# P in a PSUM bank of its own and filled one step ahead, and ScalarE copying all of the solved values, in the scan of an RWKV-7 encoder

## The chip, the cores and the metric

The kernel runs on one core of a Trainium2 chip. The metric is the device time in microseconds (us) of one execution; three runs of the kernel before gave 3077.28, 3080.88 and 3091.75, so the median is 3080.88 us. Lower is better.

The core has five engines that run side by side, each through its own list of instructions in a fixed order: TensorE (PE in the rows; PEld is its weight load), VectorE (DVE), ScalarE (ACT), GpSimd (POOL), and SyncE (SP), which issues the DMAs. TensorE writes its results into PSUM, which has eight banks of 128 partitions by 512 fp32 values.

## The reference

Two encoder layers over two requests, a prompt of 512 tokens and a sample of 256, model width 1024. Layer 0 mixes with a window attention and a short convolution, layer 1 with a bidirectional RWKV-7 time mixing; after each come a cross-attention to 256 memory tokens and a SwiGLU. Only the time mixing of layer 1 is touched. Its core is a recurrence with a 64 x 64 state for each of 16 heads and two directions:

```
def wkv7_scan(r, w, k, v, a, b, reverse):
    def step(state, inp):
        rt, wt, kt, vt, at, bt = inp
        sa = jnp.einsum('bhij,bhj->bhi', state, at)
        state = state * wt[:, :, None, :] + sa[..., None] * bt[:, :, None, :] + vt[..., None] * kt[:, :, None, :]
        return state, jnp.einsum('bhij,bhj->bhi', state, rt)
    ...
for d in range(2):
    ...
    outs.append(wkv7_scan(r, decay, k_d, v, -kk, kk * a, reverse=(d == 1)))
y = outs[0] + outs[1]
```

## The kernel before

The scan is done by chunks of 64 tokens. Inside a chunk the recurrence is a triangular system that is solved by products; from chunk to chunk a state S is handed on. The work of the time mixing is cut into 12 units (L1113): eight of the prompt, each two heads over 512 tokens, and four of the sample, each four heads over 256 tokens. A unit goes through four generators: `prep` (L1158) makes the decayed keys and values, `inverse` (L1260) and `merge` (L1329) make the masked products of keys G and the inverses X, `scan` (L1358) runs the recurrence, `tail` (L1474) normalizes. `weave` (L1514) interleaves the scan of unit u with the inverse of u+1, the tail of u-1 and the prep of u+2.

A unit's scan has eight steps (four groups i, two steps j). Both directions are worked at once. In step (i, j):

- P (128 x 128, in PSUM) is the share of the values, four matmuls of G with uv (L1424), plus the share of the state, two matmuls of AR with S0 (L1427). The four go first and the first two of them start the sum.
- ScalarE copies P into R (L1431). Two matmuls multiply R by the inverse X into U (L1433), the solved values.
- U goes back into uv in two halves: ScalarE copies partitions 0 to 63 (L1434), then VectorE partitions 64 to 127 (L1435).
- Four matmuls of BT with uv give Z (L1442), and VectorE adds Z to the decayed state and so makes the next state S1 (L1447; L1449 in a first step). GpSimd decays that for the step after (L1466).
- Matmuls of uv with G and of S0 with AR add to the output y (L1453, L1457).

P, U and Z are slices of one PSUM tile C (L1419). All these matmuls are recorded in the helper `mm` (L1389), which is the line that rows give. The next step's P therefore starts only when C is free, and that is when VectorE has read Z.

PSUM is full: two banks for the matrix products that fill (pool `fmm`, L1585), two for the pool pg (its tiles g0 and g1), and one each for pc (C), pe, py and pp (L1586). In `inverse`, a group's eight matmuls of keys go alternately to g0 and g1 (L1273), and VectorE multiplies each bank by a mask into G (L1276). Two products of the inverse and two of the merge use g1 and g0 in turn.

What keeps TensorE busy beside the chain of a step is a generator `fill` (L1532): dense matrix products of layer 0's feed-forward and of the time mixing's own projections (L342 to L344), poured in by `pour` (L1373) three times in a step, at a rate that the table FILL (L31) sets for each unit. The order of each engine's list is not written out: a scheduler takes instructions when its own model says that their inputs are there, and `urgent` (L1382) gives those of the chain the highest priority. A change of a few lines so gives a new order for the whole stretch.

Of the kernel before, what the change touches and what calls it, by code (L numbers as in the profile page):

```python
# [9 lines left out]
F32 = mybir.dt.float32  # L10
# [29 lines left out]
class Net:  # L40
# [1067 lines left out]
    def mixer1_scan(self, L, Ld, rkv, zs, bvs, fill):  # L1108

        nc, a, ph = self.nc, self.a, self.ph  # L1110
# [8 lines left out]
        NG = 4  # L1119
# [140 lines left out]
        def inverse(u, o):  # L1260
# [4 lines left out]
            st = steps[units[u][0]]  # L1265
            for i in range(NG):
                gt = ph.tile([128, 2, 2, 2, 128], F32, name="G", bufs=7)
                ps = [self.pg.tile([128, 2, 2, 128], F32, name=f"g{h}") for h in range(2)]
                for j in range(2):
                    for d in range(2):  # L1270
                        c = st[2 * i + j][d]
                        for h in range(2):
                            nc.tensor.matmul(ps[h][:, j, d, :], lhsT=flat(BK[d][lohi[h], c]), rhs=flat(AR[d][lohi[h], c]),  # L1273
                                             start=True, stop=True)
                for h in range(2):
                    nc.vector.tensor_mul(gt[:, :, h], ps[h], self.tri.unsqueeze(1).to_broadcast([128, 2, 2, 128]))  # L1276
                o["G"].append(gt)
                for q in range(4):
                    d, f = q // 2, (q % 2) * 32
                    qs = slice(32 * q, 32 * q + 32)  # L1280
                    nc.scalar.copy(XL[qs, 4 * i:4 * i + 4, :].rearrange("p (s h) i -> p s h i", h=2),
                                   gt[qs, :, :, d, 64 * d + f:64 * d + f + 32])
                yield
# [11 lines left out]
            for k in range(14, 0, -1):  # L1295
                n = 15 - k
# [6 lines left out]
            for a in range(2):  # L1303
# [7 lines left out]
            o["Y"] = Y  # L1311
            four = lambda v: ((slice(32 * q, 32 * q + 32), G[v // 4][32 * q:32 * q + 32, v // 2 % 2, v % 2, q // 2, 32 * q:32 * q + 32],
                               (32 * q, 32 * q)) for q in range(4))
            ps = self.pg.tile([128, 16, 32], F32, name="g1")
            for v in range(16):
                for qs, g, at in four(v):
                    nc.tensor.matmul(ps[qs, v, :], lhsT=g, rhs=X1[qs, v, :], start=True, stop=True, tile_position=at)
            nc.scalar.copy(Y, ps)
            yield
            ps = self.pg.tile([128, 16, 32], F32, name="g0")  # L1320
            for v in range(16):
                for qs, g, at in four(v):
                    nc.tensor.matmul(ps[qs, v, :], lhsT=Y[qs, v, :], rhs=XL[qs, v, :], start=True, stop=True, tile_position=at)
# [5 lines left out]
        def merge(u, o):  # L1329

            X1, G, Y = o["X1"], o["G"], o["Y"]
            X = o["X"]
            for q in (1, 3, 0, 2):
                qs = slice(32 * q, 32 * q + 32)
                nc.scalar.copy(X[qs, :, qs], XL[qs])
            yield
            yield
            ps = self.pg.tile([128, 16, 32], F32, name="g1")
            for v in range(16):
                i, j, h = v // 4, v // 2 % 2, v % 2  # L1340
                for d in range(2):
                    nc.tensor.matmul(ps[quart(d, 1), v, :], lhsT=G[i][quart(d, 0), j, h, d, quart(d, 1)],
                                     rhs=X1[quart(d, 0), v, :], start=True, stop=True,
                                     tile_position=(64 * d, 64 * d + 32))
            for d in range(2):
                nc.scalar.copy(Y[quart(d, 1)], ps[quart(d, 1)])
            yield
            ps = self.pg.tile([128, 16, 32], F32, name="g0")
            for v in range(16):
                for d in range(2):  # L1350
                    nc.tensor.matmul(ps[quart(d, 0), v, :], lhsT=Y[quart(d, 1), v, :],
                                     rhs=X[quart(d, 1), v, quart(d, 1)], start=True, stop=True,
                                     tile_position=(64 * d + 32, 64 * d))
            for d in range(2):
                nc.scalar.copy(X[quart(d, 0), :, quart(d, 1)], ps[quart(d, 0)])
            yield

        def scan(u, o):  # L1358
# [51 lines left out]
            fresh = [True, True]  # L1410
            nxt = ahead(0)
            yield
            for i in range(NG):
                uv, bt = nxt
                for j in range(2):
                    s0, s1, ch, before, after = st[2 * i + j]
                    cd = (s0, s1)
                    S0 = state.get(ch)
                    C = self.pc.tile([128, 384], F32, name="C")  # L1419
                    P, U, Z = C[:, 0:128], C[:, 128:256], C[:, 256:384].rearrange("p (d v) -> p d v", d=2)  # L1420
                    with urgent():
                        for h in range(2):
                            for d in range(2):
                                mm(P[lohi[d], lohi[h]], G[i][:, j, h, d, lohi[d]], uv[:, j, d, lohi[h]], h == 0)  # L1424
                        if before:
                            for d in range(2):
                                mm(P[lohi[d]], AR[d][:, cd[d], d, :], S0[:, d, :])  # L1427
                    pour()
                    with urgent():
                        R = ph.tile([128, 128], F32, name="R", bufs=1)  # L1430
                        nc.scalar.copy(R, P)  # L1431
                        for h in range(2):
                            mm(U[:, lohi[h]], X[:, 4 * i + 2 * j + h, :], R[:, lohi[h]])  # L1433
                        nc.scalar.copy(uv[lohi[0], j, 0, :], U[lohi[0]])  # L1434
                        nc.vector.tensor_copy(uv[lohi[1], j, 1, :], U[lohi[1]])  # L1435
                    pour()
                    yield
                    with urgent():
# [110 lines left out]
    def mixer1(self, l=1):  # L1549
        tc, nc = self.tc, self.nc  # L1550
        with tc.tile_pool(name="spill", bufs=1, space=bass.MemoryType.DRAM) as dram:
# [23 lines left out]
            with tc.tile_pool(name="lora", bufs=1, side="right") as lora, \  # L1575
# [4 lines left out]
                with tc.tile_pool(name="tail", bufs=1, side="right", reuse_waits="tile") as self.tl, self.phase(), ExitStack() as c:  # L1580
# [2 lines left out]
                    L[1].update(Ld[1])  # L1583
                    pool = lambda name, bufs: c.enter_context(tc.tile_pool(name=name, bufs=bufs, space=PSUM, reuse_waits="tile"))
                    f.pmm = f.psm = pool("fmm", 2)  # L1585
                    for n in ("pg", "pc", "pe", "py", "pp"):  # L1586
                        setattr(self, n, pool(n, 1))
                    y = self.mixer1_scan(L, Ld, rkv, zs, bvs, self.fill(l, f, xsave, rkv, L, zs))

# [158 lines left out]
```

## Time and profile before

| what | value |
|---|---|
| median of three runs | 3080.88 us |
| the profiled execution | 3081.32 us, its span 3079.5 us |
| mean granted TensorE clock | 0.967 of full speed |
| TensorE busy (matmul) | 2920.3 us, 95% of the span |
| VectorE busy | 1731.7 us, 56% |
| ScalarE busy | 1303.3 us, 42% |
| GpSimd busy | 679.5 us, 22% |

The page has TensorE busy nearly everywhere, so the few places where it is idle, and what ended each idle time, tell more than the shares. A busy TensorE is not one at its peak: matmuls overlap and their ends are modelled, and at a granted clock of 0.5 the same work takes longer. The steps of the scan stand between 1370 and 2275 us: the last value copies start at 2272 us.

### The profile page before, as it was taken

The numbers are of one execution on the slowest core, as the hardware profiler recorded it, in microseconds if no ns is written. First come the engines' busy times: TensorE is split into PE (matmuls) and PEld (weight loads), VectorE is DVE, ScalarE is ACT, GpSimd is POOL, SyncE is SP. The second block draws the span as 40 slices with busy tenths as digits, with TensorE's granted clock in tenths as the row PEclk, the third lists the DMA queues.
The fourth block names the chain that finished last, engine by engine and source line by source line (L and its number), as shares of the span: only waits on it lengthen the run. The fifth ranks groups of instructions, "written<-read, shape, count | busy, mean of one in ns | idle before, by whom it ended". The sixth has DMA issues, their size and how long they took to land. (4 is left out here: it accounts for less than half of the span.)

```text
span 3079.5 us, 56085 instructions
## 1 busy us (share of the span) xinstructions
PE 2920.3 (95%) x22616; PEld 2494.0 (81%) x22616; DVE 1731.7 (56%) x3074; ACT 1303.3 (42%) x2588; POOL 679.5 (22%) x672
## 2 busy tenths in 40 slices
PE   7999999999999989889989999999989999999997
PEld 6888888888888878778877877777778888888886
DVE  8888647464354586455566556555436464334244
ACT  3333435242232376455555666556445332122122
POOL 3123004010000110232356334445345010000001
PEclk9999999999999999989886998999999999999999
DMA  4234332111365767754433654222352211212121
GB/s 126 57 84 134 111 126 84 62 56 55 108 203 186 225 194 245 234 175 145 139 107 93 188 172 119 78 78 87 115 185 71 66 42 63 75 55 69 55 69 55
DMA packets 367843, 353.45 MB, mean 115 GB/s; under 512 B 43616, under 2 KB 296672, under 8 KB 367584
## 3 DMA queue, kind: packets, MB, share of 16 engines
q1 hardware_dynamic: 367584, 349.88, 36.7%
q8 instruction: 177, 2.90, 0.4%
q14 instruction: 82, 0.67, 0.1%
HBM read 272.21 MB, written 72.88 MB: 112 GB/s over the span
## 5 line engine op out<-in xcount | busy, mean ns | idle before, releaser
L342 PE MATMUL mm<-xs,whi 128*128 128x512 f32 x2128 | 748.4, 354 | 13.2 <-ACT whi L271 11.1
L343 PE MATMUL mm<-xs,whi 128*128 128x512 f32 x2128 | 752.5, 354 | 2.8 <-DVE xs L230 2.3
L344 PE MATMUL mm<-xs,wlo 128*128 128x512 f32 x2128 | 747.5, 352 | 4.2 <-DVE wlo L272 4.1
L271 ACT CAST whi<-wraw 128x512 fp32r<-128x512 f32 (+1 forms) x492 | 301.9, 616 | 841.5 <-PE mm L343 789.0
L272 DVE TENSOR_TENSOR wlo<-wraw,whi 128x512 fp32r<-128x512 f32 (+1 forms) x492 | 365.6, 745 | 393.0 <-ACT whi L271 373.6
L342 PEld LDWEIGHTS mm<-xs,whi 128*128 128x128 f32 x2128 | 403.6, 190 | 71.0 <-ACT whi L271 11.5
L344 PEld LDWEIGHTS mm<-xs,wlo 128*128 128x128 f32 x2128 | 402.1, 189 | 61.6 <-DVE wlo L272 5.7
L343 PEld LDWEIGHTS mm<-xs,whi 128*128 128x128 f32 x2128 | 403.7, 190 | 57.3 <-DVE xs L230 3.2
L194 POOL TENSOR_TENSOR acc<-acc,sq 128x768 f32<-128x768 f32 (+2 forms) x72 | 114.6, 1592 | 1264.0 <-issue 896.0
L343 PE MATMUL mm<-fb,thi 128*128 128x256 f32 (+1 forms) x720 | 234.3, 326 | 1.2 <-issue 1.0
L342 PE MATMUL mm<-hid,whi 128*128 128x512 f32 (+1 forms) x528 | 186.1, 355 | 2.3 <-ACT hid L226 2.3
L343 PE MATMUL mm<-hid,whi 128*128 128x512 f32 (+1 forms) x528 | 187.6, 356 | 0.0
L344 PE MATMUL mm<-hid,wlo 128*128 128x512 f32 (+1 forms) x528 | 186.2, 354 | 0.0
L303 ACT CAST thi<-traw 128x512 fp32r<-128x512 f32 (+1 forms) x202 | 122.8, 610 | 128.2 <-PE mm L343 51.8
L342 PE MATMUL mm<-fb,thi 128*128 128x256 f32 x528 | 166.0, 315 | 10.1 <-ACT thi L303 9.3
L344 PE MATMUL mm<-fb,tlo 128*128 128x256 f32 x528 | 159.7, 304 | 10.5 <-DMA tlo<-low 8.0
L343 PEld LDWEIGHTS mm<-fb,thi 128*128 128x128 f32 x720 | 144.8, 201 | 5.7 <-DVE fb L227 0.5
L342 PE MATMUL mm<-fa,thi 128*128 128x512 f32 (+1 forms) x304 | 125.4, 414 | 3.6 <-ACT fa L226 1.2
L342 PEld LDWEIGHTS mm<-fb,thi 128*128 128x128 f32 x528 | 107.4, 204 | 18.2 <-ACT thi L303 12.5
L344 PEld LDWEIGHTS mm<-fb,tlo 128*128 128x128 f32 x528 | 107.0, 203 | 18.0 <-DMA tlo<-low 10.5
L344 PE MATMUL mm<-fa,tlo 128*128 128x512 f32 (+1 forms) x304 | 111.7, 368 | 2.6 <-DMA tlo<-low 2.6
L342 PEld LDWEIGHTS mm<-hid,whi 128*128 128x128 f32 x528 | 99.5, 189 | 17.7 <-ACT hid L226 2.7
(386 smaller groups left out, 5830.1 us busy)
## 6 DMA issues: line engine op xcount, KB each, us to landing
wraw<-in_ffn_wgu_dram SPq DMA_DIRECT2D x44, 1024.0 KB, 5.2
tlo<-low SPq DMA_DIRECT2D x128, 256.0 KB, 3.6
low<-wlo SPq DMA_DIRECT2D x120, 256.0 KB, 3.0
wraw<-in_ffn_wdown_dram SPq DMA_DIRECT2D x23, 1024.0 KB, 5.2
traw<-in_ffn_wgu_dram SPq DMA_DIRECT2D x56, 256.0 KB, 4.0
wraw<-in_ab_w_in_dram SPq DMA_DIRECT2D x24, 512.0 KB, 3.9
wraw<-in_ca_wkv_dram SPq DMA_DIRECT2D x8, 1024.0 KB, 5.5
kvd<-kv SPq DMA_DIRECT2D x32, 256.0 KB, 2.0
```

The source lines that it names most:

```text
L194: nc.gpsimd.tensor_add(acc, acc, sq)
L271: nc.scalar.copy(hi[:, :, :m], raw[:, k0:k1, j:j + m])
L272: nc.vector.tensor_sub(lo[:, :, :m], raw[:, k0:k1, j:j + m], hi[:, :, :m].bitcast(F32))
L303: nc.scalar.copy(hi[:, :n], raw[:, :n])
L342: nc.tensor.matmul(ps[:, s0:s1], lhsT=wh, rhs=xh[:, s0:s1], start=start and k == 0, stop=False)
L343: nc.tensor.matmul(ps[:, s0:s1], lhsT=wh, rhs=xl[:, s0:s1], start=False, stop=False)
L344: nc.tensor.matmul(ps[:, s0:s1], lhsT=wl, rhs=xh[:, s0:s1], start=False, stop=stop and k == n - 1)
```

## The change

P leaves the tile C and gets a pool pP with one bank. The four matmuls of the values' share are put into a function `part0` and are issued one step ahead, behind the two matmuls that make U, so that at the turn of a step only the two matmuls of the state's share are left. The bank comes from pool pg, which now has one tile name, g: a group's eight matmuls of keys go in two lots of four, each followed by its masking multiply, and all products of the inverse and the merge share that bank. Both halves of U are copied by ScalarE. In the code after, `mm` is L1388, `part0` L1412 to L1418, and the copies are L1435 (R), L1438 and L1439 (uv).

```
@@ inverse
             for i in range(NG):
                 gt = ph.tile([128, 2, 2, 2, 128], F32, name="G", bufs=7)
-                ps = [self.pg.tile([128, 2, 2, 128], F32, name=f"g{h}") for h in range(2)]
-                for j in range(2):
-                    for d in range(2):
-                        c = st[2 * i + j][d]
-                        for h in range(2):
-                            nc.tensor.matmul(ps[h][:, j, d, :], lhsT=flat(BK[d][lohi[h], c]), rhs=flat(AR[d][lohi[h], c]),
+                for h in range(2):
+                    ps = self.pg.tile([128, 2, 2, 128], F32, name="g")
+                    for j in range(2):
+                        for d in range(2):
+                            c = st[2 * i + j][d]
+                            nc.tensor.matmul(ps[:, j, d, :], lhsT=flat(BK[d][lohi[h], c]), rhs=flat(AR[d][lohi[h], c]),
                                              start=True, stop=True)
-                for h in range(2):
-                    nc.vector.tensor_mul(gt[:, :, h], ps[h], self.tri.unsqueeze(1).to_broadcast([128, 2, 2, 128]))
+                    nc.vector.tensor_mul(gt[:, :, h], ps, self.tri.unsqueeze(1).to_broadcast([128, 2, 2, 128]))
@@ inverse and merge, in four places (g1 or g0 before)
-            ps = self.pg.tile([128, 16, 32], F32, name="g1")
+            ps = self.pg.tile([128, 16, 32], F32, name="g")
@@ scan
             nxt = ahead(0)
             yield
+            def part0(i, j, uv):
+
+                P = self.pP.tile([128, 128], F32, name="P")
+                for h in range(2):
+                    for d in range(2):
+                        mm(P[lohi[d], lohi[h]], G[i][:, j, h, d, lohi[d]], uv[:, j, d, lohi[h]], h == 0)
+                return P
+            P = part0(0, 0, nxt[0])
             for i in range(NG):
...
-                    C = self.pc.tile([128, 384], F32, name="C")
-                    P, U, Z = C[:, 0:128], C[:, 128:256], C[:, 256:384].rearrange("p (d v) -> p d v", d=2)
+                    C = self.pc.tile([128, 256], F32, name="C")
+                    U, Z = C[:, 0:128], C[:, 128:256].rearrange("p (d v) -> p d v", d=2)
                     with urgent():
-                        for h in range(2):
-                            for d in range(2):
-                                mm(P[lohi[d], lohi[h]], G[i][:, j, h, d, lohi[d]], uv[:, j, d, lohi[h]], h == 0)
                         if before:
                             for d in range(2):
                                 mm(P[lohi[d]], AR[d][:, cd[d], d, :], S0[:, d, :])
...
                         for h in range(2):
-                            mm(U[:, lohi[h]], X[:, 4 * i + 2 * j + h, :], R[:, lohi[h]])
+                            mm(U[:, lohi[h]], X[:, 4 * i + 2 * j + h, :], R[:, lohi[h]], h == 0)
                         nc.scalar.copy(uv[lohi[0], j, 0, :], U[lohi[0]])
-                        nc.vector.tensor_copy(uv[lohi[1], j, 1, :], U[lohi[1]])
+                        nc.scalar.copy(uv[lohi[1], j, 1, :], U[lohi[1]])
+                        if j == 0:
+                            P = part0(i, 1, uv)
+                        elif i + 1 < NG:
+                            P = part0(i + 1, 0, nxt[0])
@@ mixer1
-                    for n in ("pg", "pc", "pe", "py", "pp"):
+                    for n in ("pg", "pP", "pc", "pe", "py", "pp"):
                         setattr(self, n, pool(n, 1))
```

The built lists show where the change puts these instructions. First TensorE in the scan of a prompt unit, before, at the turn of a step (C is the step's tile, uv its values, S the state, ar the decayed keys; mm, fa and thi are fill):

```order
L343 MATMUL mm_15593<-fa_11438,thi_15582 128x256
L344 MATMUL mm_15593<-fa_11438,tlo_15583 128x256
L1389 MATMUL C_15632<-uv_15451,G_14134 64x64 x4
L1389 MATMUL C_15632<-S1_11408,ar0_13201 64x128
L1389 MATMUL C_15632<-S1_11408,ar1_13696 64x128
L342 MATMUL mm_15639<-fa_11437,thi_15596 128x256
```

The same step of the same unit after, where its U is made (C from R and the inverse Xinv) and the step after next to it (P_15683):

```order
L1404 MATMUL e_15810<-ident_149,bk1_13709 128x128
L1388 MATMUL C_15660<-R_15677,Xinv0_11405 128x64 x2
L1388 MATMUL P_15683<-uv_15478,G_14151 64x64 x4
L342 MATMUL mm_15688<-fa_11440,thi_15666 128x256
L343 MATMUL mm_15688<-fa_11440,thi_15666 128x256
L344 MATMUL mm_15688<-fa_11440,tlo_15667 128x256
```

The four matmuls of the values' share stood between the state and the state's share; now the next step's four stand right behind U. Next VectorE before, in front of the copy of that same step's values (xr, lt2 and lane belong to the inverse of the next unit, fa and fb to the fill, kka and bk to the prep):

```order
L448 TENSOR_TENSOR fa_11443<-fa_11443,mm_15659 128x256
L1304 TENSOR_SCALAR lane_15359<-xr_15361,lanes_11363 128x16x16 x2
L448 TENSOR_TENSOR fa_11444<-fa_11444,mm_15673 128x256
L1234 SCALAR_TENSOR_TENSOR kka_16008<-th_15972,kk_15100 128x512
L1305 STREAM_TRANSPOSE XL0_11404<-lane_15359 128x16x2x16
L227 TENSOR_TENSOR fb_15904<-fa_11443,fb_15904 128x256
L300 TENSOR_TENSOR traw_15935<-traw_15935,gmu_11342 128x512
L1235 SCALAR_TENSOR_TENSOR bk1_15968<-kka_16008,cu_15630 128x8x64
L1435 COPY uv_15451<-C_15632 64x128
```

And ScalarE after, around the two copies of the same values:

```order
L226 CAST fb_15923<-fa_11445 128x256
L1405 COPY BT_15809<-e_15810 128x512
L226 CAST fb_15929<-fa_11446 128x256
L1438 COPY uv_15478<-C_15660 64x128
L1439 COPY uv_15478<-C_15660 64x128
L191 ACTIVATE sq_15926<-fa_11445 128x256
```

The second half of the values has left VectorE's queue and stands directly behind the first half on ScalarE. Last TensorE after, where two lots of matmuls of keys (g_16568 and g_16662) follow each other in the one bank of pool pg, with little between them:

```order
L1273 MATMUL g_16568<-ar1_15999,bk1_15998 128x128
L1388 MATMUL y_16421<-G_15090,uv_16422 64x64 x2
L1388 MATMUL C_16700<-uv_16422,BT_16428 64x64 x4
L1388 MATMUL y_16421<-G_15090,uv_16422 64x64 x2
L1388 MATMUL y_16421<-ar0_14292,S0_11410 128x64
L1388 MATMUL y_16421<-ar1_14817,S0_11410 128x64
L1273 MATMUL g_16662<-ar0_15390,bk0_15389 128x128
```

The same place before has the two lots in different banks:

```order
L1273 MATMUL g1_16530<-ar0_15364,bk0_15363 128x128
L1273 MATMUL g1_16530<-ar1_15969,bk1_15968 128x128
L1273 MATMUL g1_16530<-ar0_15364,bk0_15363 128x128
L1273 MATMUL g1_16530<-ar1_15969,bk1_15968 128x128
L1273 MATMUL g0_16629<-ar0_15364,bk0_15363 128x128
```

Before, a lot in g1 is followed by one in g0; now each lot needs the bank that the masking multiply of the lot ahead has to leave first.

## Rows read from the trace of the kernel before

**Rows 1.** busy us (count) by engine, two stretches; then clock, DMA share, GB/s

```profile
1370.00:2275.00 905.00, 842.69 (x10711) 696.36 (x10708) 504.92 (x1110) 515.21 (x1216) 371.26 (x423) 0.92 0.39 116
2275.00:3079.00 804.00, 775.95 (x4506) 679.84 (x4504) 371.06 (x502) 226.86 (x386) 96.91 (x72) 0.98 0.23 73
```

**Rows 2.** TensorE's waits, 1370 to 2275 us: total us, times, longest

```profile
PE C L1389 <- DVE uv L1435: 24.8, 21, 5.6
PE C L1389 <- DVE S L1447: 11.0, 10, 2.3
PE y L1389 <- ACT uv L1434: 4.2, 8, 0.8
...
PE C L1389 <- ACT Xinv L1355: 2.9, 1, 2.9
...
PE C L1389 <- ACT R L1431: 2.0, 4, 1.0
```

**Rows 3.** VectorE in a late step: start us, us, operation

```profile
1578.95 1.74 DVE L300 TENSOR_TENSOR traw<-traw,gmu 128x512 f32<-128x512 f32 x1
1580.62 1.21 DVE L1235 SCALAR_TENSOR_TENSOR bk<-kka,cu 128x512 f32<-128x512 f32 x1
1581.86 0.29 DVE L1435 COPY uv<-C 64x128 f32<-64x128 f32 x1
```

**Rows 4.** ScalarE in the same stretch

```profile
1576.00 0.25 ACT L1434 COPY uv<-C 64x128 f32<-64x128 f32 x1
```

**Rows 5.** TensorE in the same stretch, with the idle time before and its releaser

```profile
1576.30 0.34 PE L1389 MATMUL y<-G,uv 128*64 128x64 f32 x4 [0.83 <-ACT uv L1434]
1582.21 0.38 PE L1389 MATMUL C<-uv,BT 128*64 128x64 f32 x2 [5.58 <-DVE uv L1435]
```

**Rows 6.** all engines, another step, in order of time

```profile
1845.34 0.72 ACT L1252 ACTIVATE kh<-th,par 128x512 fp32r<-128x512 f32 x1 [2.17 <-POOL th L1249]
1845.96 0.24 ACT L1434 COPY uv<-C 64x128 f32<-64x128 f32 x1
...
1846.88 0.29 DVE L1435 COPY uv<-C 64x128 f32<-64x128 f32 x1
...
1847.23 0.59 PE L1389 MATMUL C<-uv,BT 128*64 128x64 f32 x6 [2.93 <-DVE uv L1435]
```

**Rows 7.** groups, 1370 to 2275 us: count | busy, mean ns | idle, releasers

```profile
L1273 PEld LDWEIGHTS g<-ar,bk 64*128 64x128 f32 x704 | 85.2, 212 | 18.3 <-issue 10.2 <-DVE G L1276 0.9 <-DVE w2l L1192 0.7
...
L1276 DVE TENSOR_TENSOR G<-g,tri 128x512 f32<-128x512 f32 x88 | 58.8, 688 | 56.1 <-PE g L1273 52.7 <-PE y L1389 2.7
...
L1447 DVE TENSOR_TENSOR S<-C,Sd 64x128 f32<-64x128 f32 x128 | 36.8, 288 | 33.4 <-PE C L1389 30.7
...
L1435 DVE COPY uv<-C 64x128 f32<-64x128 f32 x96 | 28.3, 295 | 86.6 <-ACT uv L1434 84.5
...
L1431 ACT COPY R<-C 128x128 f32<-128x128 f32 x95 | 24.8, 261 | 68.6 <-PE C L1389 68.0
...
L1434 ACT COPY uv<-C 64x128 f32<-64x128 f32 x96 | 24.5, 255 | 42.5 <-PE C L1389 42.3
```

**Rows 8.** TensorE at the turn of a step, in order of time

```profile
1504.32 0.45 PE L1389 MATMUL C<-uv,G 128*64 128x64 f32 x8 [1.35 <-DVE S L1447]
1504.57 0.42 PE L1389 MATMUL C<-S,ar 128*64 128x128 f32 x4
```

**Rows 9.** TensorE's fill matmuls behind the wait that ended at 1582 us

```profile
1584.29 0.41 PE L343 MATMUL mm<-fa,thi 128*128 128x256 f32 x1
1584.50 0.41 PE L344 MATMUL mm<-fa,tlo 128*128 128x256 f32 x1
```

**Rows 10.** TensorE's fill matmuls later

```profile
1602.01 0.28 PE L343 MATMUL mm<-fb,thi 128*128 128x256 f32 x1
1602.13 0.28 PE L344 MATMUL mm<-fb,tlo 128*128 128x256 f32 x1
```

**Rows 11.** the engines around that wait, columns as in Rows 1

```profile
1580.00:1604.00 24.00, 19.04 (x378) 16.47 (x380) 13.88 (x25) 9.13 (x20) 10.50 (x16) 0.70 0.25 68
```

More of the change, by code (lines that the diff above doesn't have):

```diff
@@ L1319, in inverse @@
             yield
-            ps = self.pg.tile([128, 16, 32], F32, name="g0")
+            ps = self.pg.tile([128, 16, 32], F32, name="g")
             for v in range(16):
@@ L1337, in merge @@
             yield
-            ps = self.pg.tile([128, 16, 32], F32, name="g1")
+            ps = self.pg.tile([128, 16, 32], F32, name="g")
             for v in range(16):
@@ L1347, in merge @@
             yield
-            ps = self.pg.tile([128, 16, 32], F32, name="g0")
+            ps = self.pg.tile([128, 16, 32], F32, name="g")
             for v in range(16):
```

## The prediction

> **What bounds the kernel now.** I read the busy time by stretches first. In the 905 us that hold the steps of the scan, TensorE is busy 842.7 us, so it is idle for 62.3; VectorE and ScalarE are busy 505 and 515 us, a little over half [rows 1]. TensorE is the engine that sets the end, and the list of its work is nearly the same after the change. What an edit in the scan can give directly is therefore some part of those 62 us, or a better granted clock: the mean there is 0.92, against 0.98 in the 804 us behind it [rows 1].
>
> Then I read who ended TensorE's idle time. The largest entry by far is VectorE's copy of the second half of the solved values: 21 waits, 24.8 us, the longest 5.6. Next come VectorE's state addition with 11.0 us in 10 waits, and ScalarE's copies with 4.2 (values), 2.9 (inverse) and 2.0 (R) [rows 2].
>
> Then the timeline of the longest wait, to see why the copy is late. ScalarE's half starts at 1576.00 and takes 0.25 us [rows 4]; VectorE's half starts only at 1581.86 [rows 3], and TensorE, which had run out of work at 1576.63, goes on at 1582.21 [rows 5]. VectorE was not waiting: other work stood in front of the copy, the last two pieces with 1.74 and 1.21 us [rows 3]. So the copy is not slow (295 ns on average [rows 7]); its queue is long. In another step ScalarE's half is itself late, behind a 0.72 us activation, and VectorE's copy adds less than a microsecond to a wait of 2.93 [rows 6].
>
> **The change part by part.** Times are against the profiled execution, 3081.32 us (span 3079.5), which is 0.44 above the median of the runs.
>
> *The second half of the values goes to ScalarE.* 96 copies of 295 ns leave VectorE, 28.3 us in all, and 96 of some 255 ns come to ScalarE, where they stand directly behind the first half in the built order; 96 x 0.255 is 24.5 us [rows 7]. In the longest wait the second half would then end at 1576.00 + 0.25 + 0.26 = 1576.51 in place of 1582.15, before TensorE needs it, and all 5.58 us go [rows 3 to 5]. In the other step it would end at 1846.46 in place of 1847.17: 0.7 of 2.93 us go and 2.2 stay [rows 6]. Done so for the 21 waits, 16.9 us go. Bounds: nothing, and all 24.8. I take -17.
>
> *What that does to the other users of the two engines.* ScalarE gets 5% more work in this stretch, and TensorE's waits on it are 4.2 + 2.9 + 2.0 = 9.1 us [rows 2]. If they grow in proportion that is half a microsecond; if each of the 96 copies delayed something that TensorE waits for at once, it is 24.5. I take +2, near the low end, because ScalarE is busy 515 of 905 us. VectorE loses 5.6% of its work; its state additions, 11.0 us of waits, gain between 0 and 11, and I take -1.
>
> *The values' share of P moves one step ahead.* Its matmuls took 0.25 us between the wait for the state and the first matmul of the state's share [rows 8]. The work stays on TensorE and so costs the same where TensorE is not idle. Where it waits, at the state (10 times), at the values (what is left of 21) or at R (4 times), 0.25 us of work now stands ahead of the wait, or is off the chain behind it. That is worth at most 35 x 0.25, about 8.8 us, and nothing where another wait comes next. I take -2. The state's share no longer needs the bank that VectorE reads Z from, but that read is the addition which makes the state, so no wait is added or taken there. The next P needs the bank that R was copied from, and U, which stands in front of it, has waited for R already: no new wait.
>
> *One bank for the products of keys.* There are two lots of four matmuls to each group, 96 lots in all, and each has to wait until the mask multiply of the lot ahead has left the bank. That multiply takes 0.69 us [rows 7]; with the hand-over I count 0.73. Before, a wait for it cost TensorE's weight loads 0.9 us in the whole stretch [rows 7], since eight matmuls could go before a bank came round. In the built order there are mostly a dozen or more other matmuls between two lots, some microseconds of work; in eleven places at most seven rows of the list, as in those shown with the change. Bounds: 0, and 96 x 0.73 = 70 us if every turn lay open. I take +1, since the scheduler has put work between and the nearest row, 0.9, is a wait for the same multiply. The inverse's and the merge's products already need the copy of the product ahead as their input, so one bank costs them nothing.
>
> *The clock.* Behind the 5.58 us wait, fill matmuls of 256 columns start 0.21 us apart [rows 9], where later they start 0.12 apart [rows 10]: TensorE ran at 1.2 GHz for about 16 us and then again at 2.4. The 24 us around it have a mean granted clock of 0.70 and 19.0 us of busy TensorE [rows 11]. With that wait gone I expect the drop to go as well, which is worth some half of 16 us; the other waits are shorter and I put no more on them. Other drops in this stretch come without such a wait and will fall anew in another order. A mean of 0.92 over 905 us is 145 us at the lower level [rows 1]; half of that lost again or won is 36 us either way. I take -6.
>
> Sum: -17 + 2 - 1 - 2 + 1 - 6 = -23 us, and 3081.3 - 23 = 3058.
>
> **Rivals.** *The wait moves to ScalarE (no change).* For it: ScalarE's queue makes the first half late too [rows 6], its waits for U's matmuls and its own busy time are as large as VectorE's, and a new order brings waits of its own; 24.8 us spread over 21 steps can come back as many small ones. Against it: VectorE's delays in the long wait come from instructions of over a microsecond [rows 3], and the two copies on ScalarE follow each other. If three quarters of the 23 us come back, the time is 3075.
>
> *The single bank of keys sets the pace (slower).* Its place is TensorE's list in the inverse, its price 0.73 us a turn when VectorE is free, and VectorE is busy 505 of 905 us [rows 1], so a multiply may start late. If two thirds of the 96 turns lay open, that is +47, and with the -23 of the rest the time is 3105. It decides from about a third open (23 us). Against it stand the matmuls that the order puts between the lots and the 0.9 us of now [rows 7]. Beside this: the Trainium skill, in PSUM — Partial Sum Buffer, Summary: rules for kernel authors, says to give matmuls a different bank from the one that is being read; by that rule alone the change takes away in the inverse what it gives to P. TensorE: Matmul & The Clock Gate, A second HAM failure mode: psum-queue depth-cycling, tells of a kernel in which cycling through banks left small idle times between groups of matmuls and the clock fell again and again. By that, the open turns would cost clock as well; the drop in the rows above followed one long wait, so the trace before neither bears it out nor excludes it.
>
> *The clock gains more.* If the stretch got 0.96 where it has 0.92, 36 us would go in place of the 6 that I count: 3058 - 30 = 3028. For it: long waits and a drop stand together in the trace [rows 5, 9]. Against it: only one wait is that long.
>
> *The change doesn't do what it says* is excluded by the order: the four matmuls stand behind U, and the copies stand together.
>
> **How the numbers follow.** A measurement of this kernel can tell about 0.5% (15 us) from no change. Chances: the forecast 0.50 (3043 to 3070, centre 3058), the wait that moves 0.29 (3068 to 3090), the bank 0.11, the clock 0.10. Faster by over 0.5% means below 3065.5: nearly all of the clock's 0.10 and 0.43 of the forecast, 0.53. Slower by over 0.5% means above 3096.3: 0.10 of the bank's and 0.01 of the rest, 0.11. Within 0.5%: 0.36. For 8 in 10 the range has to take in most of the forecast and of the moved wait and the nearer half of the clock: 3030 to 3090.
>
> **What would show it.** In the profile after, the entry of TensorE's waits for the second copy of the values (now on ScalarE) should be at most 8 us in the stretch of the steps, and the idle total below 45. Waits of the keys' matmuls or their weight loads on the mask multiply should stay under 3 us; 20 or more would be the bank. The state addition's waits should stay near 10. TensorE's busy time should fall only where the granted clock rises; the mean clock of the stretch should be 0.92 or more. I am wrong if ScalarE's copies become the largest wait with 15 us or more, or if the clock falls below 0.90 and eats what the waits gave.

## The result, and the profile after

The change made the kernel slightly slower. Its median is 3106.39 us over 19 runs (3087.38 to 3113.12), that of before 3084.36 over 19 runs on the same chip; the ratio is 1.0071 with a 95% interval of [1.0055, 1.0088]. The forecast was 3058 and faster; the time lies above its range too. A second set of runs of the unchanged kernel gave 1.0079 [1.0056, 1.0103].

The profiled execution took 3087.38 us (span 3085.6), the fastest of the 19, so its trace shows only 6 of the 22 us that the medians are apart. The same stretch of steps as in [rows 1], same columns:

```profile
1370.00:2275.00 905.00, 856.14 (x10666) 708.55 (x10662) 488.17 (x1011) 542.90 (x1299) 363.32 (x419) 0.92 0.39 115
2280.00:3085.00 805.00, 776.53 (x4512) 680.92 (x4510) 368.40 (x502) 228.35 (x388) 96.38 (x72) 0.98 0.23 73
```

TensorE's idle time fell from 62.3 to 48.9 us, but its busy time rose from 842.7 to 856.1 at the same clock of 0.92, and the stretch is longer in spite of that. The waits of TensorE after, 1370 to 2280 us (total us, times, longest), against [rows 2]:

```profile
PE P L1388 <- DVE S L1455: 10.7, 11, 2.4
PE g L1316 <- DVE X L1306: 7.0, 4, 2.3
PE mm L342 <- ACT fa L226: 3.3, 2, 2.1
PE C L1388 <- ACT Xinv L1354: 3.2, 3, 2.6
...
PE y L1388 <- ACT uv L1438: 2.8, 6, 0.9
...
PE C L1388 <- ACT R L1435: 2.5, 5, 0.8
PE g L1273 <- DVE G L1275: 1.5, 2, 1.1
```

The 24.8 us for the second copy are gone: its line, now L1439, ends no wait. The state addition stands where it was, and the mask multiply, which now has to free the only bank of keys, costs 1.5 us. New is the wait for X, which VectorE makes for the inverse; with the copy alone and two banks it is 5.8 us (e1_act_copy below), so it is not the single bank's. The idle total stays above the 45 us that the forecast named as a sign. So the waits did for the most part what was forecast, and the time did not. The busy time says where to look: groups of TensorE over the whole execution (count | busy us, mean ns | idle, releasers), first before, then after.

```profile
L1273 PE MATMUL g<-ar,bk 64*128 64x128 f32 x768 | 113.4, 319 | 0.0
L1389 PE MATMUL C<-R,Xinv 128*128 128x64 f32 x384 | 59.7, 280 | 5.0 <-ACT Xinv L1355 2.9 <-ACT R L1431 2.0
L1389 PE MATMUL C<-uv,G 128*64 128x64 f32 x768 | 45.9, 242 | 13.8 <-DVE S L1447 11.0 <-DVE uv L1435 1.8
```

```profile
L1273 PE MATMUL g<-ar,bk 64*128 64x128 f32 x768 | 123.3, 303 | 2.0 <-DVE G L1275 1.5 <-ACT Xinv L1354 0.3
L1388 PE MATMUL C<-R,Xinv 128*128 128x64 f32 x384 | 61.3, 285 | 5.7 <-ACT Xinv L1354 3.2 <-ACT R L1435 2.5
L1388 PE MATMUL P<-uv,G 128*64 128x64 f32 x768 | 47.3, 242 | 0.4 <-ACT R L1435 0.4
```

A row counts two passes of the array for each of these fp32 matmuls, so the 384 matmuls of keys stand as x768. The keys' matmuls (g) are as many as before and each is no longer, yet together they keep TensorE 10 us longer. Busy time counts neighbours that lie over each other once, so a part of the same work no longer does. I also added up, from 1240 us to the last copy of y, the time from each matmul's start to the next one's, less idle time, and gave it to the first of the two, at whatever clock was granted there. By that TensorE's work is 948.4 us before and 969.5 after: keys 106.1 to 116.1, U 44.8 to 54.1, the values' share 29.3 to 39.3, 29 us in all, of which other groups give back 8. I call such sums work below; these three terms were to be explained.

**Keys.** The two row halves of a keys' tile (h = 0 uses rows 0 to 63 of the array, h = 1 rows 64 to 127) went to two banks before. A lot of eight passes in one half, after, and the instruction behind it (start us, us):

```profile
1385.51 1.16 PE L1273 MATMUL g<-ar,bk 64*128 64x128 f32 x8
1386.60 0.50 PE L1142 MATMUL e<-la,w2h 128*128 128x512 f32 x1
```

Sixteen passes, before, where the list mixes the two halves in places:

```profile
1388.06 1.98 PE L1273 MATMUL g<-ar,bk 64*128 64x128 f32 x16
1389.96 0.39 PE L342 MATMUL mm<-fa,thi 128*128 128x256 f32 x1
```

Eight passes of one half take 1.09 us to the next start, 0.136 each; sixteen mixed ones took 1.90, less than twice 1.09. In the trace before, 127 of the 662 times that a pass of keys follows another of keys, it starts within 80 ns of it, on average by 8: two halves run at the same time. After there is not one in 663.

**U and the share.** The values' share behind U, after:

```profile
1490.86 0.55 PE L1388 MATMUL C<-R,Xinv 128*128 128x64 f32 x4
1491.34 0.45 PE L1388 MATMUL P<-uv,G 128*64 128x64 f32 x8
1491.72 0.39 PE L342 MATMUL mm<-fa,thi 128*128 128x256 f32 x1
```

U before, followed by fill:

```profile
1490.24 0.55 PE L1389 MATMUL C<-R,Xinv 128*128 128x64 f32 x4
1490.61 0.36 PE L342 MATMUL mm<-fb,thi 128*128 128x256 f32 x1
```

U to the next start is 0.37 us before and 0.48 after; the share is 0.25 before, with the state's share behind it [rows 8], and 0.38 after. Together 0.62 became 0.86. The third column names the part of the array that a matmul uses: U and the fill use 128*128, the share 128*64. Before, the share's neighbour behind it used 128*64 too; after, it stands between two 128*128, and each change of that form costs time. The whole stretch agrees: at the full clock a pass of U takes 107 ns on average to the next start when a 128*128 comes next (264 times in the trace after) and 205 when a 128*64 does (69 times). Changes from 128*128 to 128*64 rose from 149 to 229, and 80 times the 0.24 us of the example are the 19 us of the two sums.

### The profile page after: what moved, and what is told of

The parts are those of the page before. It is cut to its first block, busy times and chain, and to the rows that moved or that the text cites. A ratio compares the mean times of both kernels' runs of the same rounds, so it can differ in the third digit from the quotient of the medians.

```text
span 3085.6 us, 56108 instructions
## 1 busy us (share of the span) xinstructions
PE 2940.2 (95%) x22616; PEld 2510.5 (81%) x22616; DVE 1716.0 (56%) x2978; ACT 1336.8 (43%) x2684; POOL 677.0 (22%) x672
## 4 chain that ended last, share of the span: by engine, by line
PE 77%; DVE 10%; DMA 5%; ACT 3%; issue 3%; POOL 2%; SPq 1%; DVEq 0%; POOLq 0%; ACTq 0%
PE mm L342 20%; PE mm L343 20%; PE mm L344 19%; PE g L1273 3%; PE y L1388 2%; PE C L1388 2%; PE P L1388 2%; DMA traw<-in_ffn_wgu_dram 1%; PE mm L333 1%; PE e L1142 1%; PE sm L333 1%; DVE wlo L272 1%; DVE xs L230 1%; DVE xr L1298 1%; DVE lt L1297 1%
## 5 line engine op out<-in xcount | busy, mean ns | idle before, releaser
L1275 DVE TENSOR_TENSOR G<-g,tri 128x512 f32<-128x512 f32 x96 | 66.2, 690 | 115.7 <-PE g L1273 115.3
L1273 PE MATMUL g<-ar,bk 64*128 64x128 f32 x768 | 123.3, 303 | 2.0 <-DVE G L1275 1.5
L1273 PEld LDWEIGHTS g<-ar,bk 64*128 64x128 f32 x768 | 102.0, 203 | 21.3 <-issue 9.4
```

What stands on the lines that cost most here:

```text
L1273: nc.tensor.matmul(ps[:, j, d, :], lhsT=flat(BK[d][lohi[h], c]), rhs=flat(AR[d][lohi[h], c]), start=True, stop=True)
L1275: nc.vector.tensor_mul(gt[:, :, h], ps, self.tri.unsqueeze(1).to_broadcast([128, 2, 2, 128]))
```

## The experiments

All ratios are against the kernel before in the same set of runs, with 95% intervals. The clock is the mean granted clock of TensorE over the runs; before had 0.968 to 0.970 in the sets of runs that list it (for the 19 runs beside those of after it is not listed). Differences between two kernels in us are those of their ratios, times 3080.

| kernel | banks for keys | second copy | values' share | median us (runs) | ratio | clock |
|---|---|---|---|---|---|---|
| after | 1 | ScalarE | own bank, behind U | 3106.39 (19) | 1.0071 [1.0055, 1.0088] | 0.961 |
| e1_act_copy | 2 | ScalarE | in C | 3051.23 (6) | 0.9912 [0.9890, 0.9934] | 0.975 |
| e3_one_bank | 1 | VectorE | in C | 3111.31 (6) | 1.0114 [1.0089, 1.0139] | 0.963 |
| e11_one_bank_act | 1 | ScalarE | in C | 3098.10 (11) | 1.0052 [1.0032, 1.0072] | 0.964 |
| e2_dve_copy | 1 | VectorE | own bank, behind U | 3111.26 (6) | 1.0115 [1.0094, 1.0136] | 0.964 |
| e6_behind_z | 1 | ScalarE | own bank, behind Z | 3085.26 (12) | 1.0025 [1.0007, 1.0043] | 0.968 |
| e5_h_major | 2, half by half | VectorE | in C | 3066.17 (12) | 0.9962 [0.9939, 0.9984] | 0.971 |
| e12_alternate_dve | 2, alternating | VectorE | in C | 3058.86 (6) | 0.9931 [0.9910, 0.9952] | 0.971 |
| e7_alternate | 2, alternating | ScalarE | in C | 3025.76 (4) | 0.9840 [0.9820, 0.9861] | 0.973 |
| e10_shared_pe | 2, pe and pp one bank | ScalarE | in C | 3095.35 (6) | 1.0071 [1.0053, 1.0090] | 0.965 |
| e9_two_banks_p | 2, pe and pp one bank | ScalarE | own bank, behind U | 3149.62 (6) | 1.0228 [1.0203, 1.0253] | 0.951 |

**The copy alone** (before, one line):

```
-                        nc.vector.tensor_copy(uv[lohi[1], j, 1, :], U[lohi[1]])
+                        nc.scalar.copy(uv[lohi[1], j, 1, :], U[lohi[1]])
```

> The kernel before with one edit: ScalarE copies the second half of the values too; P stays in C, two banks for the keys. Theory (TensorE does more work after: the two row halves of the keys' matmuls no longer overlap, +10 us, and the array changes its tiling about 80 times more each way around the moved values' share, +26 us in those places): this kernel has neither, so TensorE's waits on the value copies (24.8 us) go and its work stays; 12 to 20 us faster, ratio 0.993 to 0.996. Rival (the stretches at half clock fall by luck of the order): ratio within 0.995 to 1.005, with the granted clock telling it. Rival (the second copy on ScalarE is itself the cost): ratio about 1.005, and new waits on ScalarE of 10 us or more.

0.9912, 27 us faster. TensorE's waits, 1370 to 2280 us:

```profile
PE C L1389 <- DVE S L1447: 12.3, 23, 2.2
...
PE C L1389 <- ACT uv L1435: 4.6, 5, 2.2
PE mm L342 <- ACT thi L303: 4.5, 1, 4.5
PE y L1389 <- ACT uv L1434: 3.7, 7, 1.3
PE C L1389 <- ACT R L1431: 3.6, 6, 0.8
```

The wait for the copy went from 24.8 to 4.6 us, and TensorE's waits for ScalarE's values and R are 11.9 us in all, against 6.2 before. From 1240 us on, idle time before the step's own matmuls (tiles C) fell from 41.8 to 22.5 us, but before the products of the inverse and the merge it rose from 2.9 to 10.1, so that all idle time fell by 11. The rest of the gain came with a better clock, 0.975 in place of 0.968. The edit took away the waits that the forecast named, so the loss lies in the other parts.

**The single bank alone** (before; the inverse's and the merge's products go to g as in the change):

```
-                ps = [self.pg.tile([128, 2, 2, 128], F32, name=f"g{h}") for h in range(2)]
...
+                for h in range(2):
+                    ps = self.pg.tile([128, 2, 2, 128], F32, name="g")
```

> The kernel before with one bank for the products of keys, in two lots of four; P stays in C, VectorE keeps its copy, one PSUM bank stands unused. Theory (row halves no longer overlap): the keys' matmuls go from 138 to about 150 ns start to start, +8 to +12 us of TensorE work, waits on the mask multiply stay under 3 us; ratio 1.002 to 1.005. Rival (the turns of the bank lie open): waits on the mask multiply of 20 us or more, ratio 1.007 or more. Rival (clock): no change that the rows of the keys' matmuls show.

1.0114, 35 us slower, more than I expected of it. Waits of TensorE, 1370 to 2280 us, and the group of keys:

```profile
PE C L1388 <- DVE uv L1434: 15.3, 13, 3.3
PE C L1388 <- DVE S L1446: 14.7, 11, 2.7
...
PE g L1273 <- DVE G L1275: 0.3, 1, 0.3
```

```profile
L1273 PE MATMUL g<-ar,bk 64*128 64x128 f32 x768 | 126.4, 307 | 0.6 <-DVE G L1275 0.3 <-ACT Xinv L1354 0.3
```

The keys' matmuls wait 0.3 us for the mask multiply, so the rival of open turns falls: the bank is free in time. No two passes overlap, and the keys' work is 118.9 us against 106.1. The rest of the 35 us is 11 us more idle time and more time at the lower of the clock's two levels: 184 us of the stretch from 1240 us on in place of 154. Ten of the 11 us stand before the products of the inverse and the merge, which share the one bank here; e1_act_copy has seven more there with two banks, so this too can be the order's doing.

**Was it the order of the loop?** The change also puts h outermost. Here that is done with both banks kept:

```
+                for h in range(2):
-                for j in range(2):
-                    for d in range(2):
-                        c = st[2 * i + j][d]
-                        for h in range(2):
+                    for j in range(2):
+                        for d in range(2):
+                            c = st[2 * i + j][d]
```

> The kernel before with its two banks for the keys, but the four matmuls of one row half before the four of the other in the program. Theory (overlap of row halves): most pairs that started 10 ns apart (121 of 662) go, the keys' matmuls take 5 to 8 us more, ratio 1.001 to 1.004. Rival (bank turns): there are two banks, so nothing changes, ratio 1.000, and the mean from start to start stays near 138 ns.

0.9962 where I expected a small loss. With two banks the scheduler is free to mix the halves, and 91 pairs still overlap:

```profile
L1273 PE MATMUL g<-ar,bk 64*128 64x128 f32 x768 | 109.6, 304 | 1.4 <-DVE G L1276 1.3 <-POOL ar L1230 0.2
```

The loop order is the same as in e3_one_bank and the intervals are far apart: with this loop it is the one bank, with what it does to the built order, that makes the loss. But a new order alone brought 12 us here, with a clock of 0.971 and fewer overlaps than before, so not every microsecond of such a difference is the overlap's.

**The values' share in another place.** Read as above, the share should cost nothing behind Z, whose matmuls use 128*64 as it does (after; held there):

```
-                        if j == 0:
-                            P = part0(i, 1, uv)
...
+                        with tc.issue_after(last[0].ins):
+                            if j == 0:
+                                P = part0(i, 1, uv)
```

> The kernel after with the values' share queued behind the four matmuls of Z in place of behind U: both have the same tiling of the array, so the built list has 667 changes of tiling in place of 822. Theory (changes of tiling): 15 to 25 us less than after, ratio to before 0.998 to 1.002; the changes from the full array to the half-width tiles fall from 229 to about 150 and take about 17 us less. Rival (clock, or the one bank alone): stays with after, ratio 1.005 to 1.008.

1.0025, 14 us below the changed kernel, the intervals apart. Its groups and its timeline:

```profile
L1388 PE MATMUL C<-R,Xinv 128*128 128x64 f32 x384 | 62.0, 287 | 5.8 <-ACT R L1435 2.9 <-ACT Xinv L1354 2.7
L1388 PE MATMUL P<-uv,G 128*64 128x64 f32 x768 | 42.9, 232 | 0.0
```

```profile
1472.04 0.55 PE L1388 MATMUL C<-R,Xinv 128*128 128x64 f32 x4
1472.40 0.37 PE L342 MATMUL mm<-fb,thi 128*128 128x256 f32 x1
...
1527.57 0.45 PE L1388 MATMUL C<-uv,BT 128*64 128x64 f32 x8
1527.86 0.40 PE L1388 MATMUL P<-uv,G 128*64 128x64 f32 x8
1528.09 0.29 PE L1388 MATMUL y<-G,uv 128*64 128x64 f32 x4
```

U is back at 0.36 us, and between Z and y the share takes 0.23 where it took 0.38; the sums follow: U 47.5 us (54.1), the share 28.5 (39.3). The place cost what the forms cost in these two sums. The time is not made of them alone: from after to here all work falls by 30 us, idle time rises by 18, and 24 us less are at the lower clock.

**Held alternation.** If overlapping halves are what a second bank is worth, more of them should pay. With the copy on ScalarE, the eight matmuls are chained so that h = 0 and h = 1 alternate:

```
+                prev = None
...
                         for h in range(2):
-                            nc.tensor.matmul(ps[h][:, j, d, :], ...
+                            with tc.issue_after(prev.ins) if prev else nullcontext():
+                                prev = nc.tensor.matmul(ps[h][:, j, d, :], ...
```

> The kernel of e1_act_copy with the keys' matmuls held in an order in which the two row halves alternate (283 turns from one half to the other in the built list, 113 in e1). Theory (matmuls of the two row halves overlap only when two banks let them alternate): overlapped starts (under 80 ns apart) rise from 160 to about 350 of 768, the keys' matmuls fall from 94 to about 75 us, TensorE's granted clock is 0.975 or more, time 3035 to 3048, ratio 0.985 to 0.990. Rival (the overlap does not matter, one bank costs by its waits): same as e1, 0.991.

0.9840, the best time of the study and better than both kernels, though the clock is 0.973 and not the 0.975 that I expected. In the timeline and the group:

```profile
1392.04 1.16 PE L1275 MATMUL g<-ar,bk 64*128 64x128 f32 x16
1393.13 0.40 PE L342 MATMUL mm<-fa,thi 128*128 128x256 f32 x1
```

```profile
L1275 PE MATMUL g<-ar,bk 64*128 64x128 f32 x768 | 81.5, 313 | 0.0
```

Sixteen passes now take the 1.09 us that eight took after. There are 332 overlaps (160 in e1_act_copy), the keys' work falls from 93.9 to 74.5 us, and all work from 929.4 to 909.7: all of the work that went is the keys'.

The alternation without the copy (the same edit in before):

```
+                            with tc.issue_after(prev.ins) if prev else nullcontext():
```

> The kernel before with nothing changed but the order of the keys' matmuls, held so that the two row halves alternate; VectorE keeps its copy. Theory (overlap): overlapped starts rise from 127 to over 300, the keys' matmuls fall from 106 to 75 to 85 us, 20 to 35 us faster, ratio 0.989 to 0.994. Rival (e7's gain over e1 is luck of the order): within 0.4% of before, whatever the overlap.

0.9931; 326 overlaps, keys 72.8 us. The two parts add: 0.9912 x 0.9931 is 0.9844, and both together measured 0.9840.

**The copy back on VectorE** (after):

```
-                        nc.scalar.copy(uv[lohi[1], j, 1, :], U[lohi[1]])
+                        nc.vector.tensor_copy(uv[lohi[1], j, 1, :], U[lohi[1]])
```

> The kernel after with VectorE's copy of the second half again: P's bank and its share one step ahead, one bank for the keys. Theory (the ScalarE copy is the gain, worth 25 us in e1): slower than after by 10 to 25 us, ratio 1.010 to 1.015, waits of 10 us or more on VectorE's value copy. Rival (ScalarE's copy adds to the loss): at or below after's 1.007.

1.0115, the same as the single bank alone, so the own bank for P moved nothing there; the copy is worth 14 us in this company, against 27 alone.

**One bank and the copy, P in C** (e3_one_bank with the copy on ScalarE):

```
-                        nc.vector.tensor_copy(uv[lohi[1], j, 1, :], U[lohi[1]])
+                        nc.scalar.copy(uv[lohi[1], j, 1, :], U[lohi[1]])
```

> The kernel before with one bank for the keys and ScalarE's second copy, P not moved: after without P's move. Theory (one bank costs about 33 us, the ScalarE copy gives 27, P's move behind U costs TensorE work that its saved waits do not pay): 3078 to 3095 us, ratio 1.001 to 1.005, so after's P move is worth a loss of 5 us or more, and U's matmuls take 117 to 120 ns start to start as in e1, not 141. Rival (P's move pays as forecast): slower than after, ratio 1.008 or more.

1.0052, just above what I expected: against e1_act_copy the bank costs 43 us. U's matmuls take 129 ns from start to start, between the 117 of e1_act_copy and the 141 of after. The step from here to the changed kernel, the move of P alone, is +6 us with intervals that overlap.

**A bank from elsewhere.** Could P have its bank without taking it from the keys? First only the pools of the transposes (pe) and of the prep (pp) are made one, in e1_act_copy:

```
-                    for n in ("pg", "pc", "pe", "py", "pp"):
+                    for n in ("pg", "pc", "pe", "py"):
                         setattr(self, n, pool(n, 1))
+                    self.pp = self.pe
```

> The kernel of e1_act_copy with the transposes and the preparation in one bank, one bank unused: the cost of that sharing alone. Theory: 3055 to 3070 us, ratio 0.992 to 0.997; e9 minus this is P's move. If P's move were worth what was forecast, e9 would be 2 to 8 us faster than this.

1.0071, where I expected 0.992 to 0.997: the gain of the copy is lost, 49 us above e1_act_copy. Then P gets the bank, in the changed kernel with both banks of keys back:

```
-                    for n in ("pg", "pP", "pc", "pe", "py", "pp"):
+                    for n in ("pg", "pP", "pc", "pe", "py"):
                         setattr(self, n, pool(n, 1))
+                    self.pp = self.pe
```

> The kernel after, but the keys have their two banks again, and P's bank comes from the transposes, which share one bank with the preparation. Theory (the loss is the keys' lost bank): overlapped starts are back (over 120), ratio below after's by 0.7% or more, 0.995 to 1.001, held back by 924 changes of tiling in the built list and by the shared bank. Rival (the moved values' share and its changes of tiling are the loss): stays at 1.005 to 1.010. Against e10, which shares the same two banks without moving P, it tells what P's move is worth.

1.0228, the slowest kernel here, against my expectation of about no change. Its share of the values:

```profile
L1389 PE MATMUL P<-uv,G 128*64 128x64 f32 x768 | 59.3, 258 | 10.3 <-ACT uv L1400 9.9
```

Its changes of form are 924 (768 before, 822 after), U and the share make 103 us of work (80 in e10_shared_pe), and 225 us of its stretch are at the lower clock. Of the 48 us against e10_shared_pe, some 11 are work at the full clock and none is idle time, by the table below; the rest goes with the lower clock, and what lowered it was not separated from the order that comes with the move.

**The changed kernel once more**, unchanged, in the hope of a profile at the typical time:

> The kernel after unchanged, for a second profile. Theory: its span lies nearer the median of 3106 than the first profile's 3085.6, with the same TensorE work within 10 us and the difference in the stretches at half clock. Rival: the difference lies in a wait that the first profile missed.

1.0079, but the profiled execution had a span of 3085.0 us again, the fastest of its 8. So no trace shows one of the typical runs, and what follows on their clock rests on the clock that each run lists, not on a timeline.

**The work without the clock.** The sums of work mix two things, what TensorE does and the clock that it is granted. Here each interval is weighed with the granted clock at its time (0.5 or 1), from 1240 us to the last copy of y, in the profiled execution. What that takes off the work is the share of the lower clock. This is an estimate, good to some 5 us: at the lower clock a fill matmul takes 0.21 us where it takes 0.12 at the full one [rows 9, 10], a little less than double.

| kernel | work at the full clock, us | of it keys | U and the share | lower clock | idle |
|---|---|---|---|---|---|
| before | 877 | 91 | 68 | 72 | 86 |
| after | 897 | 105 | 86 | 72 | 72 |
| e1_act_copy | 878 | 87 | 71 | 52 | 75 |
| e3_one_bank | 885 | 106 | 70 | 86 | 97 |
| e11_one_bank_act | 882 | 106 | 72 | 92 | 86 |
| e2_dve_copy | 897 | 105 | 85 | 73 | 88 |
| e6_behind_z | 879 | 105 | 69 | 61 | 89 |
| e5_h_major | 883 | 95 | 69 | 45 | 80 |
| e12_alternate_dve | 857 | 70 | 70 | 58 | 92 |
| e7_alternate | 851 | 68 | 70 | 59 | 73 |
| e10_shared_pe | 884 | 85 | 74 | 66 | 87 |
| e9_two_banks_p | 895 | 82 | 89 | 108 | 84 |

The stretch as the profile gives it, columns as in [rows 1], for before, e1_act_copy, e11_one_bank_act and e9_two_banks_p; the third number from the end is the clock:

```profile
1240.00:2275.00 1035.00, 949.08 (x11741) 791.47 (x11740) 574.06 (x1255) 583.26 (x1355) 407.83 (x463) 0.93 0.43 129
1240.00:2244.00 1004.00, 929.17 (x11740) 775.20 (x11739) 556.96 (x1159) 612.77 (x1449) 402.95 (x463) 0.95 0.44 133
1240.00:2300.00 1060.00, 973.66 (x11737) 812.26 (x11736) 556.22 (x1158) 617.24 (x1449) 397.98 (x463) 0.91 0.42 126
1240.00:2328.00 1088.00, 1003.60 (x11742) 825.72 (x11741) 556.11 (x1158) 619.14 (x1450) 404.33 (x463) 0.90 0.41 122
```

Keys cost 105 or 106 us wherever they have one bank and 68 to 95 with two; U and the share cost 85 to 89 where the share stands behind U and 68 to 74 elsewhere. These two follow the edits. The share of the lower clock does not follow the number of banks: it is 45 to 108 us with two and 61 to 92 with one. A profiled execution need not be a typical one, either: that of e5_h_major is the fastest of its 12.

## Why the prediction was wrong

*The second copy: right in its mechanism, its size in part luck.* Forecast -17, with +2 and -1 beside it and -6 of clock; the copy alone measures -27 us, -19 and -14 beside a single bank. The long wait went, ScalarE's load made no large new one (the rival of the moved wait, 3075, is not what happened), and the state addition kept its 11 to 12 us, as forecast. But idle time fell by 11 us only, since the inverse waited more; some 20 of the 30 us between the two profiles are the clock's, where -6 was forecast.

*The single bank of keys: this step failed.* "I take +1, since the scheduler has put work between and the nearest row, 0.9, is a wait for the same multiply." It measures +35 us alone and +43 beside the copy. The reason given holds, as the waits of 0.3 to 1.5 us show; what it left out is that two banks let two row halves run at once. In before 127 passes did so, at 0.136 us each some 17 us of TensorE's time at the full clock; the keys' work rose by 14 (91 to 105), and by 19 from e1_act_copy to e11_one_bank_act. That much is shown to be the overlap's, since it follows it up and down: no overlap 105, 127 overlaps 91, 332 overlaps 68. The rest of the +35 and +43 is idle time (some 11 us each) and the lower clock (some 14 and 40 us in the profiles); that the lost overlap causes these is not shown, as a new order alone can move them. The sum took it that the work on TensorE stays as it is, and bounded only waits. A row that hints at it stood in the trace before: sixteen passes in 1.90 us, 0.119 each; that eight of one half take 1.09 is a row of after. The slower rival gave 3105, and 3106 came, but by luck: its turns lay shut.

*The values' share: wrong in its ground, small in its effect.* "The work stays on TensorE and so costs the same" is false: U and the share together cost 19 us more behind U than in before, by the changes of form, and the state's share, now without them in front, 3 more. Against this stands less idle time, 71.7 us from 1240 us on against 86.3 in e11_one_bank_act, more than the 8.8 that the forecast had as its bound. Beside one bank the move measures between 0 (e3_one_bank to e2_dve_copy) and +6 us in place of -2. Behind Z it may pay: e6_behind_z is at 1.0025, e11_one_bank_act at 1.0052, but their intervals overlap a little.

*The clock: wrong sign in the timed runs.* Forecast -6. The profiled stretch has 0.92 as before. But the 19 runs average 0.961, and in the second set of runs the same kernel has 0.962 where before has 0.968. Within a kernel, over all runs, 0.001 of mean clock goes with about 2.3 us; by that some 14 of the 22 us go with the clock. The others are about what the two profiles show, both of executions at 0.967: work at the full clock +20, idle -14. The kernels with one bank for keys have 0.961 to 0.968, most with two 0.968 to 0.975, but e9_two_banks_p and e10_shared_pe have two and 0.951 and 0.965, so this is a correlation at most. What lowers the clock was not settled. The forecast also took the drop of the clock there as following the long wait. The engines just before that wait and in it, columns as in [rows 1]:

```profile
1572.00:1576.60 4.60, 3.66 (x29) 3.03 (x27) 4.53 (x14) 4.32 (x13) 2.86 (x4) 1.00 0.78 231
1576.60:1582.20 5.60, 0.03 (x2) 0.00 (x0) 5.54 (x9) 2.72 (x6) 4.34 (x4) 0.58 0.55 154
```

A mean of 0.58 over the wait means that the clock fell to its lower level about a microsecond after the wait began. The wait's length of 5.6 us is thus no measure of what made it fall.

The steps from before to after, the copy -27, the bank +43, P's move +6, come to the +22 us of the ratio 1.0071 by the way that they are taken, each from the kernel of the last, so their sum proves nothing. In another order the bank is +35, the copy -19 and P's move +6, or the bank +35, P's move 0 and the copy -14. In each, the bank is the only large loss.

## What to carry to other kernels

Before a bank is taken from a group of matmuls, look at whether its neighbours overlap: compare the time to the next start of a run of passes with that of one pass times their number. Work that "only moves" is priced anew by its neighbours, so put matmuls beside others that use the same part of the array. And where halves can run at once, holding the order that alternates them can be worth nearly as much as the largest wait that a profile lists (here -21 us, against -27 for the copy).

## What the runs showed of the hardware

Passes with 64 rows on opposite halves of the array, into different banks, ran fully side by side in e7_alternate: sixteen in 1.09 us, the time of eight of one half in after. Halving the banks with the same loop order took overlaps from 91 to 0; whether two halves could overlap in one bank was not tried, since the lots there never alternate. A change from 128*128 to 128*64 or back cost 0.11 to 0.13 us at the full clock (U 0.37 to 0.48, the share 0.25 to 0.38). And the same kernel is granted another mean clock from one run to the next, 0.961 to 0.976 in before, with times from 3064 to 3095 us, so that one profiled execution need not stand for the median.
